# Weight folds moved into the first cross attention, the last down products over all PSUM banks, and Fourier blocks in another order

## The chip, the cores and the metric

One core of one Trainium2 chip runs the whole program in one launch. The metric is the device time of one execution in microseconds (us). The kernel before took 2213.67 us as the median of 3 runs (2210.46 to 2213.92). Engines are named as in the profile: PE is TensorE, DVE is VectorE, ACT is ScalarE, POOL is GpSimd, and SP (SyncE) issues every DMA of this kernel.

## The reference, cut to what matters

Two requests (512 and 256 tokens, width 1024) pass through two layers with the same weights. Each layer is a mixer, a cross attention over 256 memory tokens and a gated feed-forward part; layer 0's mixer is differential attention, layer 1's is a Fourier mixing.

```python
def fourier_mix(xn, w_in, w_out):
    u = (xn @ w_in).reshape(B, S, FNET_GROUPS, FNET_GROUP_DIM)
    f = jnp.fft.fft2(u, axes=(1, 3), norm="ortho").real
    return f.reshape(B, S, D_MODEL) @ w_out

def conv_glu(xn, w_up, conv_w, conv_b, w_down):
    gate, val = jnp.split(xn @ w_up, 2, axis=-1)
    gate = dwconv3(gate, conv_w, conv_b)          # 3 taps over time
    return (jax.nn.gelu(gate) * val) @ w_down

for i in range(2):
    x = x + mixer[i](rmsnorm(x, norm_mix_g[i]))
    x = x + cross_attention(rmsnorm(x, norm_xattn_g[i]), rmsnorm(mem, norm_mem_g[i]), ...)
    x = x + conv_glu(rmsnorm(x, norm_ffn_g[i]), ...)
return rmsnorm(x, final_norm_g)
```

## The kernel before, in words

Activations lie with channels on the partitions: 8 chunks of 128 channels by 768 tokens (both requests side by side, GROUPS = 512 and 256). Every float32 operand is split into a high and a low part, and a product is three matmuls (`mm3`, L150 to L155: high by high, low activation, low weight). A split is one ACT cast for the high part and one DVE subtraction for the low part (`load_w`, L147 and L148; `split`, L186 and L187).

The program is written in the order of the stages, and a scheduler then sets the order of the instructions on each engine from that order, from the buffers of each pool and from its own estimates. Each engine, and SP's DMA queue, works its list off in order: an instruction that waits holds all behind it.

The stages, in order: attention; cross attention 0 (`xq` queries, `xs` scores, `xt` transposes, `xav` values); its output product with the residual (`ob`, function `residual`); feed-forward 0 (`fp`, `fg`, `fv` up products, `fd` down products); the Fourier stage; cross attention 1; its output product; feed-forward 1, which ends in the final norm.

A feed-forward part takes its 22 hidden chunks in four blocks (6, 6, 6, 4). `prepare` loads the two up weights of a chunk and forms weight sums in tiles of tag `S` (two buffers, `s23` and `s14`) so that 7 quarter products do the work of 8. `first_half`, `rest` and `close` run these products and end in the hidden chunk (`hh`, `hl`). After a block come its down products, 8 output chunks `n` in each of the two token groups. In the first three blocks `fd` uses the two banks of tag `s`, and the result is scaled by DVE (`t`, L633) and added by POOL (`xs`, L634). In the last block (`last`), all eight weights are loaded ahead, the 512-token group is done for n = 0 to 7 and then the 256-token group; each result goes to `xr` (L629), and `each` squares it for the statistics of the next norm. For layer 0 `each` also starts to fold the activations for the Fourier stage (`into_mixer`, DVE ops `xm`, `eo`, `x3l`); for layer 1 it writes the output (`into_output`, L1270). The PSUM banks of this stage are b1, b2, b3 and s, two each; the statistics and their broadcast (`pt`, `pbmix`, `pbfin`) take banks of tag `s` too.

The weights of the Fourier stage are folded on the chip: sums and differences of left and right halves go to DRAM. `fold_weights` (L943 to L993) is a generator with 16 units: 8 of `in_fin` (names `fw..i`) and 8 of `in_fout` (`fw..o`). A unit loads two tiles of 256 KB, adds (L985) and subtracts (L986) on DVE and stores the results; for the five parts in `FIRST` it also splits them (L963, L964). It takes its tiles from tag `S` of feed-forward 0, and one step is taken before each `down` of the first three blocks (L656).

The Fourier stage opens with three products at once (`fu00`, `fu01`, `fu10`), then loads tables, then `fu11`, then the middle column `uny`, and later `fu20` and `fu21`. These products and `uny` share four PSUM banks (tag `g`).

Of the kernel before, what the change touches and what calls it, by code (L numbers as in the profile page):

```python
# [10 lines left out]
F32 = mybir.dt.float32  # L11
# [48 lines left out]
def trunk_kernel(ctx: ExitStack, tc: tile.TileContext, a: dict):  # L60
# [286 lines left out]
    def cross_attention(layer, acts, finish, pq, po):  # L347
        with tc.tile_pool(name=f"xa{layer}", bufs=1, reuse_waits="tile") as pool:
# [82 lines left out]
            for h, u in units + [(None, None)]:  # L431
                now = None
                if h is not None:
                    if h not in heads:
                        run(fill)
                        fill = chain(query(2 * h + 2), query(2 * h + 3)) if h < XA_HEADS - 1 else iter(())
                        heads[h] = load_head(h)
                    now = h, u, softmax(h, u, heads[h][0])
                run(fill, XSLICES[0])
                if prev is not None:  # L440
                    pt = transposed(*prev)
                run(fill, XSLICES[1])
                if prev is not None:
                    values(*prev[:2], pt, heads[prev[0]][1])
                run(fill, XSLICES[2])
                prev = now
            return o
# [12 lines left out]
    class Forms:  # L460
# [17 lines left out]
        def feed(self, pool, stats, gcol):  # L478
# [29 lines left out]
    def ffn(layer, pool, forms, extra, hidp, finish, x_src, x_keep, make_last, side):  # L508
# [115 lines left out]
        def down(n, w, j0, j1, x, off, ln, last, each):  # L624
            sl = slice(off, off + ln)
            ps = pss(f"fd{layer}_{j0}{n}_{off}")
            gemm(ps[:, :ln], w, [hid(j) for j in range(j0, j1)], sl)
# [13 lines left out]
        for b, (j0, j1) in enumerate(FF_BLOCKS):  # L641
# [8 lines left out]
            if not last:  # L650
                for n in range(KC):
                    w = load(n, j0, j1)
                    x = small_tile("xs", f"xs{b}{n}", T, 2)
                    nc.sync.dma_start(out=x, in_=(x_src if b == 0 else x_keep)[n])
# [266 lines left out]
    def attend_and_feed(layer, acts, finish, x_in, p_in, p_alt, make_last):  # L921


        with banks(f"xa{layer}", g=4, c=2, s=2):
            o = cross_attention(layer, acts, finish, p_alt, p_in)
            outer = ffn_pools[layer].enter_context(tc.tile_pool(name=f"ffo{layer}", bufs=1, reuse_waits="tile"))
            extra = lambda name, dtype=F32R: outer.tile([P, T], dtype, tag="xe", name=f"{name}{layer}", bufs=10)
            xe = [extra(f"xe{i}_") for i in range(10)]
            st = Stats(f"f{layer}")
            forms = Forms(layer, p_alt, p_in, xe)  # L930
            with tc.tile_pool(name=f"xo{layer}", bufs=1, reuse_waits="tile") as pool:
                residual(lambda name: pool.tile([P, T], F32, tag="xr", name=name, bufs=3), f"ob{layer}_",
                         lambda n: a["xo"][layer, n], o, lambda n: x_in[n], x2_scr[layer],
                         forms.feed(pool, st, V_FFN + 8 * layer))
        with ffn_pools[layer], banks(f"ffn{layer}", b1=2, b2=2, b3=2, s=2):
            pool = ffn_pools[layer].enter_context(tc.tile_pool(name=f"ffn{layer}", bufs=1, reuse_waits="tile"))
            hidp = [(page(p_in, f"hh{layer}_{i}"), page(p_in, f"hl{layer}_{i}")) for i in range(7)]
            return ffn(layer, pool, forms, extra, hidp, st.finish, x2_scr[layer], x2_scr[layer], make_last,
                       iter(()) if layer else fold_weights(pool))

    ffn_pools = [ExitStack(), ExitStack()]


    FIRST = ((0, 0), (0, 1), (1, 0), (1, 1), (2, 0))

    def fold_weights(pool):

        def pair(name, shape):
            t = pool.tile([P, KC, P], F32, tag="S", name=f"fw{name}", bufs=2)
            return t[:, :KC // 2], t[:, KC // 2:]  # L950

        def load(name, left, right):
            shape = list(left.shape)
            l, r = pair(f"lr{name}", shape)
            nc.sync.dma_start(out=l, in_=left)
            nc.sync.dma_start(out=r, in_=right)
            return l, r

        def keep(t, hi, dst, parts):
            if parts is None:  # L960
                return [(dst, t)]
            hi = hi.bitcast(F32R)
            nc.scalar.copy(out=hi, in_=t)  # L963
            nc.vector.tensor_tensor(out=t.bitcast(F32R), in0=t, in1=f32(hi), op=ALU.subtract)  # L964
            move(parts[0], hi)
            return [(parts[1], t)]
# [12 lines left out]
        yield  # L979
        now = load(units[0][0], *units[0][3])  # L980
        yield
        for k, (name, dst, parts, _) in enumerate(units):
            l, r = now
            e, hi = pair(f"e{name}", list(l.shape))
# [3 lines left out]
            stores = keep(e, hi, dst[0], parts[0]) + keep(l, r, dst[1], parts[1])  # L988
            yield
            for to, t in stores:  # L990
                move(to, t)
            if k + 1 < len(units):
                now = load(units[k + 1][0], *units[k + 1][3])  # L993
# [65 lines left out]
    with banks("fnet", g=4, s=4):  # L1059
        with tc.tile_pool(name="fnet", bufs=1, reuse_waits="tile") as pool:  # L1060
# [70 lines left out]
            mixed_in(1, 1)  # L1131
# [71 lines left out]
            mixed_in(2, 0)  # L1203
# [184 lines left out]
```

## Time and profile before

| | |
|---|---|
| median of 3 runs | 2213.67 us |
| profiled execution, its own time | 2211.7 us |
| its span | 2209.9 us |
| PE busy | 2077.9 us (94%) |
| DVE busy | 1372.8 us (62%) |
| ACT busy | 898.5 us (41%) |
| POOL busy | 576.1 us (26%) |
| granted TensorE clock, mean | 0.972 |

The busy time of an engine counts its instructions, not its issue of DMAs or its waits. The granted clock is 1 at TensorE's upper level (2.4 GHz) and 0.5 at the lower (1.2 GHz); a value between is a mean over a stretch. Times in rows are us from the start of the span.

### The profile page before, as it was taken

To read this page: it belongs to the slowest core of one execution; us is meant where nothing else is said; L and a number is where in the kernel's file an instruction comes from. 1 tells how busy PE (TensorE), PEld (TensorE's weight loads), DVE (VectorE), ACT (ScalarE), POOL (GpSimd) and SP (SyncE) were. 2 spreads that over 40 slices of the span, in tenths; PEclk is the share of its full clock that TensorE was granted. 3 is DMA by queue.
4 is the path that set the end of the run, shared out by engine and by line. 5 is a ranking of instruction groups with operands and counts; after the bars stand their busy time and mean duration, and the time that the engine had idled before them with its cause. 6 is when DMAs were issued, how large, how long until landed. Compare 5 with 4: busy or idle time off the path is not lost.

```text
span 2209.9 us, 32686 instructions
## 1 busy us (share of the span) xinstructions
PE 2077.9 (94%) x12455; PEld 1911.6 (87%) x12455; DVE 1372.8 (62%) x2226; ACT 898.5 (41%) x1550; POOL 576.1 (26%) x467
## 2 busy tenths in 40 slices
PE   7999999999999999928999987999999999999996
PEld 5898889799898899828999886889989989999895
DVE  6445777775435688537658466473567847748564
ACT  4324555554325455204325243353445524425232
POOL 5543222221200431202132324020033223142233
PEclk9999999999999999968999999999999999999997
DMA  5775686775532322752342454354242243241441
GB/s 185 211 228 166 209 261 210 246 243 202 191 104 93 118 91 73 262 209 86 129 158 72 134 168 142 127 185 149 77 146 82 72 141 110 79 169 67 133 154 62
DMA packets 151517, 328.35 MB, mean 149 GB/s; under 512 B 15680, under 2 KB 57792, under 8 KB 151360
## 3 DMA queue, kind: packets, MB, share of 16 engines
q1 hardware_dynamic: 151360, 326.26, 44.5%
q8 instruction: 98, 1.61, 0.3%
q14 instruction: 59, 0.48, 0.1%
HBM read 236.28 MB, written 89.92 MB: 148 GB/s over the span
## 4 chain that ended last, share of the span: by engine, by line
PE 47%; DVE 5%; DMA 3%; ACT 1%; issue 1%; POOL 1%; SPq 0%; DVEq 0%; POOLq 0%; ACTq 0%
PE fd L153 5%; PE fp L162 4%; PE fd L155 4%; PE fp L163 4%; PE fd L154 4%; PE fp L164 4%; PE fv L162 2%; PE fv L163 2%; PE fv L164 2%; PE fg L162 1%; PE fg L163 1%; PE fg L164 1%; PE xq L153 1%; PE xq L154 1%; PE xq L155 1%
## 5 line engine op out<-in xcount | busy, mean ns | idle before, releaser
L153 PE MATMUL fd<-hh,h_d 128*128 128x256 f32 (+1 forms) x640 | 221.4, 347 | 18.6 <-ACT hh L186 11.7
L154 PE MATMUL fd<-hl,h_d 128*128 128x256 f32 (+1 forms) x640 | 216.9, 341 | 0.0
L155 PE MATMUL fd<-hh,l_d 128*128 128x256 f32 (+1 forms) x640 | 214.0, 340 | 0.6 <-DVE l_d L148 0.5
L634 POOL TENSOR_TENSOR xs<-xs,t 128x512 f32<-128x512 f32 x96 | 119.5, 1245 | 274.9 <-DVE t L633 259.9
L153 PEld LDWEIGHTS fd<-hh,h_d 128*128 128x128 f32 x640 | 121.5, 190 | 43.2 <-ACT hh L186 12.5
L633 DVE TENSOR_TENSOR t<-fd,rbcf 128x512 f32<-128x512 f32 x96 | 53.3, 556 | 151.2 <-PE fd L155 95.4
L547 POOL TENSOR_TENSOR s<-r_v 128x512 f32<-128x512 f32 x44 | 57.9, 1316 | 316.1 <-DMA r_v<-in_up 250.3
L155 PEld LDWEIGHTS fd<-hh,l_d 128*128 128x128 f32 x640 | 121.7, 190 | 16.7 <-DVE l_d L148 2.7
L154 PEld LDWEIGHTS fd<-hl,h_d 128*128 128x128 f32 x640 | 121.9, 190 | 14.4 <-DVE hl L187 1.0
L147 ACT CAST h_d<-r_d 128x768 fp32r<-128x768 f32 (+1 forms) x56 | 44.5, 803 | 203.7 <-PE fd L154 180.3
L214 POOL TENSOR_TENSOR acc_x<-acc_x,sq_x 128x512 f32<-128x512 f32 (+2 forms) x49 | 66.9, 1371 | 186.4 <-ACT sq_x L213 186.4
L214 POOL TENSOR_TENSOR acc_f<-acc_f,sq_f 128x512 f32<-128x512 f32 (+1 forms) x28 | 35.1, 1259 | 291.6 <-issue 228.1
L826 POOL TENSOR_TENSOR p<-p 128x512 f32<-128x512 f32 (+1 forms) x48 | 58.2, 1213 | 176.9 <-DVE p L824 136.4
L548 POOL TENSOR_TENSOR s<-r_g,r_v 128x512 f32<-128x512 f32 x44 | 81.6, 1854 | 78.3 <-DVE l_C L187 78.3
L162 PE MATMUL fp<-bf,h_C 128*128 128x384 f32 x264 | 88.9, 337 | 0.4 <-ACT ux L589 0.4
L164 PE MATMUL fp<-bf,l_C 128*128 128x384 f32 x264 | 89.2, 338 | 0.0
L818 ACT ACTIVATE p<-sc,mx,rs 128x512 f32<-128x512 f32 (+1 forms) x96 | 67.1, 703 | 52.6 <-DVE mx L815 52.5
L163 PE MATMUL fp<-bf,h_C 128*128 128x384 f32 x264 | 88.5, 335 | 0.0
L601 DVE TENSOR_TENSOR hs<-fp,rbcf 128x128 f32<-128x128 f32 x88 | 27.4, 354 | 92.4 <-PE fp L164 92.4
L186 ACT CAST h_B<-s 128x1024 fp32r<-128x1024 f32 x44 | 46.1, 1048 | 83.3 <-DVE s L549 55.4
L186 ACT CAST h_A<-r_g 128x1024 fp32r<-128x1024 f32 x44 | 46.3, 1052 | 82.5 <-PE fg L163 48.6
L314 PE MATMUL xv<-h_xv,mnh 128*128 128x256 f32 x256 | 74.3, 290 | 0.0
(559 smaller groups left out, 7306.4 us busy)
## 6 DMA issues: line engine op xcount, KB each, us to landing
r_g<-in_up SPq DMA_DIRECT2D x44, 512.0 KB, 3.2
r_v<-in_up SPq DMA_DIRECT2D x44, 512.0 KB, 3.2
xs<-x_scr SPq DMA_DIRECT2D x48, 384.0 KB, 3.6
r_d<-in_down SPq DMA_DIRECT2D x48, 384.0 KB, 3.3
x_scr<-xs SPq DMA_DIRECT2D x48, 384.0 KB, 2.6
qst<-q_scr SPq DMA_DIRECT2D x64, 192.0 KB, 4.9
r_xk<-in_xk SPq DMA_DIRECT2D x16, 512.0 KB, 4.6
r_xv<-in_xv SPq DMA_DIRECT2D x16, 512.0 KB, 4.3
```

Source lines behind the costliest of these rows:

```text
L153: nc.tensor.matmul(out=ps, lhsT=wh, rhs=xh, start=first, stop=False)
L154: nc.tensor.matmul(out=ps, lhsT=wh, rhs=xl, start=False, stop=False)
L155: nc.tensor.matmul(out=ps, lhsT=wl, rhs=xh, start=False, stop=last)
L162: nc.tensor.matmul(out=ps, lhsT=wh, rhs=xh, start=first and p == 0, stop=False, skip_group_check=True)
L163: nc.tensor.matmul(out=ps, lhsT=wh, rhs=xl, start=False, stop=False, skip_group_check=True)
L164: nc.tensor.matmul(out=ps, lhsT=wl, rhs=xh, start=False, stop=p == 3, skip_group_check=True)
L186: nc.scalar.copy(out=hi, in_=src)
L214: nc.gpsimd.tensor_tensor(out=self.acc[:, sl], in0=self.acc[:, sl], in1=sq[:, :n], op=ALU.add)
L314: nc.tensor.matmul(out=ps, lhsT=xh[:, ts], rhs=wh[:, kc % 4, :], start=kc == 0, stop=False)
L548: nc.gpsimd.tensor_tensor(out=s23[:, h:], in0=a11, in1=a21, op=ALU.subtract)
L634: nc.gpsimd.tensor_tensor(out=x[:, sl], in0=x[:, sl], in1=t[:, :ln], op=ALU.add)
L818: nc.scalar.activation(p[:, c, :nk], scs[c][:, :nk], AF.Exp, bias=mx[:, c:c + 1], scale=rs8[:, tq:tq + 1], accum_out=sm[:, c, qc:qc + 1])
```

## The change

Three edits, and one clean-up without effect (`x_src` was the same tensor as `x_keep`).

First, `fold_weights` gets its list of units from outside, takes four tiles of its own (`fwl`, `fwr`, `fwe`, `fwh`, one buffer each) from whichever pool it is given, and is stepped twice in each turn of cross attention 0's loop (12 units) and once per result of the output product (4 units). Feed-forward 0 no longer steps it.

Second, the last block's down products of a token group hold eight banks at once (s, s, b1, b1, b2, b3, b2, b3). In the 512-token group the first six chunks do three of their four hidden chunks first, and the last hidden chunk afterwards.

Third, in the Fourier stage `mixed_in(1, 1)` and `mixed_in(2, 0)` are called before the tables are loaded.

```diff
-            units = [(h, u) for h in range(XA_HEADS) for u in range(3)]
+            steps = [(h, u) for h in range(XA_HEADS) for u in range(3)]
+            side = fold_weights(pool, units)
+            for h, u in steps + [(None, None)]:
+                next(side, None)
...
                 run(fill, XSLICES[1])
+                next(side, None)
...
             def each(n, xn, off, ln):
                 pair = n // 2
+                next(side, None)
                 stats.add(xn[:, off:off + ln], off, ln)
...
                     for off, ln in GROUPS:
-                        next(side, None)
                         down(n, w, j0, j1, x, off, ln, False, None)
...
+            order = ("s", "s", "b1", "b1", "b2", "b3", "b2", "b3")
+            hids = [hid(j) for j in range(j0, j1)]
             for off, ln in GROUPS:
-                for n in range(KC):
-                    down(n, ws[n], j0, j1, xr[n], off, ln, True, each)
+                ps = [None] * KC
+                early = 6 if off == 0 else 0
+                for part in (0, 1):
+                    for n in range(KC):
+                        k0, k1 = (0, j1 - j0 - 1) if part == 0 else (j1 - j0 - 1, j1 - j0)
+                        if n >= early:
+                            if part == 0:
+                                continue
+                            k0 = 0
...
+                        for k in range(k0, k1):
+                            mm3(ps[n][:, :ln], (ws[n][0][:, k, :], ws[n][1][:, k, :]),
+                                [t[:, sl] for t in hids[k]], k == 0, k == j1 - j0 - 1)
+                        if part:
+                            down(n, ws[n], j0, j1, xr[n], off, ln, True, each, ps[n])
...
+        def tile_(tag, name, dtype=F32):
+            return pool.tile([P, KC // 2, P], dtype, tag=tag, name=f"{tag}{name}", bufs=1)
...
+        for name, dst, parts, src in units:
+            flush()
+            l, r = tile_("fwl", name), tile_("fwr", name)
+            nc.sync.dma_start(out=l, in_=src[0])
+            nc.sync.dma_start(out=r, in_=src[1])
+            yield
+            e = tile_("fwe", name)
             nc.vector.tensor_tensor(out=e, in0=l, in1=r, op=ALU.add)
             nc.vector.tensor_tensor(out=l, in0=l, in1=r, op=ALU.subtract)
+            keep(e, f"{name}e", dst[0], parts[0])
+            keep(l, f"{name}o", dst[1], parts[1])
             yield
...
+            mixed_in(1, 1)
+            mixed_in(2, 0)
             hid_t = table("dft_h", [NHID])
...
-            mixed_in(1, 1)
...
             hidden(0)
-            mixed_in(2, 0)
             mixed_in(2, 1)
```

What this does to the order is shown at three places. The first is SP's queue in cross attention 0, in the changed kernel; the names with `fw` are tiles of the fold, `kt` and `vt` are keys and values of a head, `r_xq` a query weight.

```order
L986 DMA fwri00_7128<-in_fin 128x512
L68 DMA kt0_00_7131<-xk_scr0_86 128x2x512
L68 DMA vt0_00_7133<-xv_scr0_88 128x4x256
L68 DMA kt0_01_7135<-xk_scr0_86 128x2x512
L68 DMA vt0_01_7137<-xv_scr0_88 128x4x256
L68 DMA fin3_scr_90<-fwhi00e_7193 128x512
L68 DMA fin3_scr_90<-fwei00_7190 128x512
L986 DMA fwri04_7207<-in_fin 128x512
L68 DMA kt0_10_7431<-xk_scr0_86 128x2x512
L68 DMA fin3_scr_90<-fwhi00o_7197 128x512
L68 DMA fin3_scr_90<-fwli00_7127 128x512
L68 DMA vt0_10_7433<-xv_scr0_88 128x4x256
```

The loads of the heads, which stood one behind another, now have stores of the fold between them, each of which waits for its DVE or ACT result.

The second is PE at the last down products of feed-forward 0; `hh0_0` and `hl0_0` are the last hidden chunk, `hh0_4` to `hh0_6` the three before it, and `fd0_180_0` to `fd0_187_0` the eight output chunks. Before:

```order
L155 MATMUL fd0_181_0_13250<-hh0_6_8756,l_d0_181_13197 128x512
L153 MATMUL fd0_180_0_13235<-hh0_0_8744,h_d0_180_13189 128x512
L153 MATMUL fd0_181_0_13250<-hh0_0_8744,h_d0_181_13196 128x512
L154 MATMUL fd0_180_0_13235<-hl0_0_8745,h_d0_180_13189 128x512
L155 MATMUL fd0_180_0_13235<-hh0_0_8744,l_d0_180_13190 128x512
L154 MATMUL fd0_181_0_13250<-hl0_0_8745,h_d0_181_13196 128x512
```

After:

```order
L155 MATMUL fd0_181_0_13271<-hh0_6_8940,l_d0_181_13223 128x512
L153 MATMUL fd0_182_0_13281<-hh0_4_8936,h_d0_182_13229 128x512
L154 MATMUL fd0_182_0_13281<-hl0_4_8937,h_d0_182_13229 128x512
L155 MATMUL fd0_182_0_13281<-hh0_4_8936,l_d0_182_13230 128x512
L153 MATMUL fd0_182_0_13281<-hh0_5_8938,h_d0_182_13229 128x512
```

Before, two output chunks are brought up to the last hidden chunk and the third matmul row shown already needs it; now chunks 182 to 185, nine matmuls each, come first. Feed-forward 1 is moved in the same way.

The third is PE in the Fourier stage, at the end of `fu11`. Before:

```order
L155 MATMUL fu11_13890<-x3h7_13181,fi3wlo_13567 128x388
L153 MATMUL uny_13919<-x3h0_13167,nywh_13880 36x388
L154 MATMUL uny_13919<-x3l0_13168,nywh_13880 36x388
L155 MATMUL uny_13919<-x3h0_13167,nywl_13881 36x388
L153 MATMUL uny_13919<-x3h1_13169,nywh_13880 36x388
```

After:

```order
L155 MATMUL fu11_13900<-x3h7_13207,fi3wlo_13593 128x388
L153 MATMUL fu20_13927<-x3h0_13193,fi4whi_13746 128x388
L154 MATMUL fu20_13927<-x3l0_13194,fi4whi_13746 128x388
L155 MATMUL fu20_13927<-x3h0_13193,fi4wlo_13747 128x388
L153 MATMUL fu20_13927<-x3h1_13195,fi4whi_13746 128x388
```

`fu20`, 24 matmuls, stands where `uny` stood, and `uny` follows it; the order of ACT's casts and of SP's loads up to there is as before.

## Rows read from the trace of the kernel before

**Rows 1.** Waits of PE: engine, line, waited for: us in total, times, longest us.

```profile
PE fp L162 <- ACT h_B L186: 46.1, 1, 46.1
PE fd L153 <- ACT hh L186: 11.7, 2, 6.1
PE fd L153 <- DVE xr L629: 5.7, 5, 1.8
```

**Rows 2.** Timeline before 1004 us: start, us, instruction [idle before <-releaser].

```profile
990.78 0.69 DVE L985 TENSOR_TENSOR fweo<-fwlro 128x512 f32<-128x512 f32 x1 [4.68 <-DMA fwlro<-in_fout]
...
997.21 0.69 DVE L985 TENSOR_TENSOR fweo<-fwlro 128x512 f32<-128x512 f32 x1 [5.01 <-DMA fwlro<-in_fout]
...
1000.30 1.26 POOL L547 TENSOR_TENSOR s<-r_v 128x512 f32<-128x512 f32 x1 [50.13 <-DMA fout_scr<-fweo]
```

**Rows 3.** Stretches, both feed-forwards: width, busy by engine (instructions), PEclk, DMA share, GB/s.

```profile
774.61:1323.62 549.01, 489.39 (x2727) 461.75 (x2728) 360.07 (x478) 198.56 (x264) 137.84 (x101) 0.94 0.41 138
1668.47:2160.04 491.57, 484.92 (x2728) 459.16 (x2728) 331.35 (x436) 192.81 (x254) 138.07 (x101) 0.99 0.34 113
```

**Rows 4.** Stretches: down products of block 0, feed-forward 0 and 1.

```profile
885.05:948.66 63.61, 57.88 (x312) 49.34 (x313) 36.85 (x51) 14.81 (x21) 18.46 (x15) 0.97 0.78 269
1779.26:1835.10 55.84, 55.66 (x314) 48.13 (x313) 23.65 (x31) 8.90 (x11) 21.42 (x17) 1.00 0.49 168
```

**Rows 5.** Stretches of cross attention 0 and of its output product.

```profile
610.00:670.00 60.00, 60.00 (x380) 54.06 (x380) 23.61 (x48) 17.80 (x39) 0.00 (x0) 1.00 0.25 87
...
680.00:690.00 10.00, 10.00 (x84) 9.69 (x83) 7.93 (x24) 6.34 (x20) 0.00 (x0) 1.00 0.29 100
...
720.00:730.00 10.00, 10.00 (x57) 8.69 (x56) 8.75 (x11) 6.32 (x9) 5.07 (x4) 1.00 0.51 187
```

**Rows 6.** DMA issues of the fold: KB each, median us from issue to landing.

```profile
fwlri<-in_fin SPq DMA_DIRECT2D x16, 256.0 KB, 3.4
...
fout_scr<-fweo SPq DMA_DIRECT2D x8, 256.0 KB, 2.1
```

**Rows 7.** Timeline of POOL and DVE in the output product.

```profile
738.20 1.33 POOL L501 TENSOR_TENSOR F<-F 128x384 f32<-128x384 f32 x1
...
738.69 1.25 DVE L502 TENSOR_TENSOR F<-F 128x384 f32<-128x384 f32 x1
...
754.02 0.56 DVE L500 TENSOR_TENSOR F<-F 128x384 f32<-128x384 f32 x1 [1.37 <-ACT F L495]
```

**Rows 8.** Timeline of DVE and PE at the last down products, feed-forward 0.

```profile
1318.63 0.69 DVE L148 TENSOR_TENSOR hl<-r_d,hh 128x512 fp32r<-128x512 f32 x1 [0.25 <-ACT hh L147]
...
1323.62 1.22 PE L153 MATMUL fd<-hh,h_d 128*128 128x512 f32 x2 [6.10 <-ACT hh L186]
...
1328.30 0.40 PE L153 MATMUL fd<-hh,h_d 128*128 128x512 f32 x1
...
1342.89 0.39 PE L153 MATMUL fd<-hh,bf 128*128 128x512 f32 x1
```

**Rows 9.** Stretches after the wait for the last hidden chunk, and of the activations' fold.

```profile
1323.62:1343.78 20.16, 20.16 (x80) 15.69 (x81) 5.78 (x8) 4.42 (x7) 7.64 (x6) 0.91 0.13 38
...
1349.77:1368.84 19.07, 10.68 (x76) 9.45 (x74) 19.06 (x34) 8.21 (x20) 5.37 (x6) 0.98 0.88 302
...
2160.04:2180.11 20.07, 20.07 (x80) 15.61 (x81) 5.78 (x8) 4.42 (x7) 7.68 (x6) 0.92 0.00 1
```

**Rows 10.** Timeline of DVE near the end of the program.

```profile
2190.00 5.36 DVE L1270 SCALAR_TENSOR_TENSOR xr<-xr,vec,pbfin 128x512 f32<-128x512 f32 x8
...
2198.44 0.42 DVE L629 TENSOR_TENSOR xr<-fd,xr 128x256 f32<-128x256 f32 x1 [2.75 <-PE fd L155]
```

**Rows 11.** Timeline of SP and PE in the Fourier stage.

```profile
1395.43 0.38 SPq L68 DMA_DIRECT2D fi4wlo<-fin_scr  x1
...
1398.29 0.36 PE L153 MATMUL uny<-x3h,nywh 128*36 128x388 f32 x1 [4.58 <-DVE ul L187]
```

**Rows 12.** DMA issues: the weight of `fu20` (KB each, us to landing).

```profile
fi4wlo<-fin_scr SPq DMA_DIRECT2D x1, 512.0 KB, 4.9
```

More of the change, by code (lines that the diff above doesn't have):

```diff
@@ L344, in feed, with cross_attention @@
         return each
-    def cross_attention(layer, acts, finish, pq, po):
+    def cross_attention(layer, acts, finish, pq, po, units=()):
         with tc.tile_pool(name=f"xa{layer}", bufs=1, reuse_waits="tile") as pool:
@@ L446, in cross_attention @@
                 prev = now
+            run(1.0 for _ in side)
             return o
@@ L476, in form, with feed @@
             return out
-        def feed(self, pool, stats, gcol):
+        def feed(self, pool, stats, gcol, side):
             f, last = {}, {}
@@ L506, in feed, with ffn @@
             return each
-    def ffn(layer, pool, forms, extra, hidp, finish, x_src, x_keep, make_last, side):
+    def ffn(layer, pool, forms, extra, hidp, finish, x_keep, make_last):
         hs_buf = []
@@ L622, in hid, with down @@
             return hidp[j % 7]
-        def down(n, w, j0, j1, x, off, ln, last, each):
+        def down(n, w, j0, j1, x, off, ln, last, each, ps=None):
             sl = slice(off, off + ln)
-            ps = pss(f"fd{layer}_{j0}{n}_{off}")
-            gemm(ps[:, :ln], w, [hid(j) for j in range(j0, j1)], sl)
+            if ps is None:
+                ps = pss(f"fd{layer}_{j0}{n}_{off}")
+                gemm(ps[:, :ln], w, [hid(j) for j in range(j0, j1)], sl)
             if last:
@@ L653, in ffn @@
                     x = small_tile("xs", f"xs{b}{n}", T, 2)
-                    nc.sync.dma_start(out=x, in_=(x_src if b == 0 else x_keep)[n])
+                    nc.sync.dma_start(out=x, in_=x_keep[n])
                     for off, ln in GROUPS:
-                        next(side, None)
                         down(n, w, j0, j1, x, off, ln, False, None)
@@ L918, in trunk_kernel, with fold_units @@
     a_banks.close()
[L921 to L941, printed above, removed]
-    FIRST = ((0, 0), (0, 1), (1, 0), (1, 1), (2, 0))
[L946 to L966, printed above, removed]
+    FIRST = ((0, 0), (0, 1), (1, 0), (1, 1), (2, 0))
+    def fold_units():
         h = KC // 2
@@ L978, in fold_weights, with flush, keep @@
                           [a["fout"][n, :, i] for i in range(2)]))
[L979 to L984, printed above, removed]
+        return units
+    def fold_weights(pool, units):
+        stores = []
+        def flush():
+            for to, t in stores:
+                move(to, t)
+            stores.clear()
+        def tile_(tag, name, dtype=F32):
+            return pool.tile([P, KC // 2, P], dtype, tag=tag, name=f"{tag}{name}", bufs=1)
+        def keep(t, name, dst, parts):
+            if parts is None:
+                stores.append((dst, t))
+                return
+            hi = tile_("fwh", name, F32R)
+            nc.scalar.copy(out=hi, in_=t)
+            nc.vector.tensor_tensor(out=t.bitcast(F32R), in0=t, in1=f32(hi), op=ALU.subtract)
+            move(parts[0], hi)
+            stores.append((parts[1], t))
+        for name, dst, parts, src in units:
[5 more added lines that the diff above has]
+            e = tile_("fwe", name)
@@ L985, in fold_weights @@
             nc.vector.tensor_tensor(out=e, in0=l, in1=r, op=ALU.add)
             nc.vector.tensor_tensor(out=l, in0=l, in1=r, op=ALU.subtract)
-            stores = keep(e, hi, dst[0], parts[0]) + keep(l, r, dst[1], parts[1])
+            keep(e, f"{name}e", dst[0], parts[0])
+            keep(l, f"{name}o", dst[1], parts[1])
             yield
[L990 to L993, printed above, removed]
+        flush()
@@ new lines, in fold_weights, with attend_and_feed @@
+        yield
+    def attend_and_feed(layer, acts, finish, x_in, p_in, p_alt, make_last):
+        with banks(f"xa{layer}", g=4, c=2, s=2):
+            units = [] if layer else fold_units()
+            o = cross_attention(layer, acts, finish, p_alt, p_in, units[:12])
+            outer = ffn_pools[layer].enter_context(tc.tile_pool(name=f"ffo{layer}", bufs=1, reuse_waits="tile"))
+            extra = lambda name, dtype=F32R: outer.tile([P, T], dtype, tag="xe", name=f"{name}{layer}", bufs=10)
+            xe = [extra(f"xe{i}_") for i in range(10)]
+            st = Stats(f"f{layer}")
+            forms = Forms(layer, p_alt, p_in, xe)
+            with tc.tile_pool(name=f"xo{layer}", bufs=1, reuse_waits="tile") as pool:
+                side = fold_weights(pool, units[12:])
+                residual(lambda name: pool.tile([P, T], F32, tag="xr", name=name, bufs=3), f"ob{layer}_",
+                         lambda n: a["xo"][layer, n], o, lambda n: x_in[n], x2_scr[layer],
+                         forms.feed(pool, st, V_FFN + 8 * layer, side))
+                run(1.0 for _ in side)
+        with ffn_pools[layer], banks(f"ffn{layer}", b1=2, b2=2, b3=2, s=2):
+            pool = ffn_pools[layer].enter_context(tc.tile_pool(name=f"ffn{layer}", bufs=1, reuse_waits="tile"))
+            hidp = [(page(p_in, f"hh{layer}_{i}"), page(p_in, f"hl{layer}_{i}")) for i in range(7)]
+            return ffn(layer, pool, forms, extra, hidp, st.finish, x2_scr[layer], make_last)
@@ L995, in load_first @@
+    ffn_pools = [ExitStack(), ExitStack()]
     def load_first(b):
```

4 lines of the change are left out of this document (3 added, 1 removed).

## The prediction

> **What bounds the kernel now.** I read the engines' shares and the slices of the span first, then the waits of PE, then stretches of the span, then the timeline around each long wait. PE is busy 94% of the span, and nearly everything outside a few places is PE-bound, so the time moves with PE's waits and with the matmuls run at the lower clock. The list of waits [rows 1] has one entry that dwarfs the rest: 46.1 us in a single wait of `fp` for the weight sum `h_B`. The timeline before it [rows 2] shows why. POOL's `s`, which `h_B` is made from, had been idle 50.13 us until a store of the fold (`fout_scr<-fweo`) had landed: the fold and `prepare` share the two buffers of tag `S`. Meanwhile the fold went one unit every 6.43 us (990.78 to 997.21), DVE waiting some 5 us of each for its load. Next come the two waits for the last hidden chunk (11.7 us, one of 6.1) and the five waits for `xr` [rows 1].
>
> **The fold out of feed-forward 0.** Feed-forward 1 runs the same products without a fold, so it prices the removal without adding waits one by one. From the first waiting `fp` matmul to the wait for the last hidden chunk feed-forward 0 takes 549.01 us and feed-forward 1 491.57, with 2727 and 2728 matmuls [rows 3]: 57.44 longer. That holds the 46.1 us, the matmuls after it at the lower clock (granted mean 0.94 against 0.99), and the disturbed down products of block 0 (63.61 against 55.84, 7.77 longer [rows 4]). 6.10 of it against some 5.6 in feed-forward 1 is the wait for the last chunk [rows 1, 8], which belongs to the second edit; so 56.9 us go.
>
> **The fold into cross attention 0.** It brings 32 additions and subtractions and 10 splits: 42 DVE instructions of 0.69 us [rows 2], 29 us, with 10 ACT casts, and 32 loads and 42 stores in SP's queue. 34 of the DVE instructions fall into the attention, 8 into the output product. What covers them: from 610 to 670 us DVE is busy 23.61 of 60 us and PE never idle [rows 5], with query products between the scores, so there I count nothing. From 680 to 690 DVE is busy 7.93 of 10 [rows 5]; the order puts about two units, four instructions, into the 20 us of that dense part: 2.8 us of work against some 4 us of idle time, which do not fall together, so I count 1 us. A unit cannot go faster than load, two DVE instructions and store (3.4 + 1.4 + 2.1 = 6.9 us [rows 2, 6]), because its one buffer must be stored before the next load; where the order puts two units closer than that, DVE holds the softmax behind a load for 1 to 2 us. I take 3 us in all. The lower bound is 0. The upper bound is the nearest place where a fold ran beside products, block 0's down products: 7.77 us for about 6.5 units [rows 4], 1.2 a unit, 19 us for 16. I stay near the low end because the down products had two PSUM banks and the queries have four, and because PE there had no idle slice at all.
>
> One rule speaks against it. In the output product a DVE instruction on two SBUF tensors took 1.25 us just after POOL's `F` began, and 0.56 us with POOL free [rows 7]. The Trainium skill, "GPSIMD Engine Reference", section "1. Specifications", says that GpSimd shares its SBUF interfaces with VectorE and contends with instructions of two SBUF inputs; the trace agrees. By it the 8 fold instructions in the output product could take 0.69 us more each, 5.5 us of DVE time in a stretch where DVE is busy 8.75 of 10 at its worst [rows 5], and the 34 in the attention nothing, as POOL does nothing there (0.00). With four banks between PE and DVE I leave it inside the bounds above.
>
> **Last down products, feed-forward 0.** Four more output chunks, 36 matmuls, now stand before the first need of the last hidden chunk. A 512-column matmul takes (1342.89 - 1328.30) / 63 = 0.232 us [rows 8], so they cover 8.3 us of a wait of 6.10. The weight of the sixth chunk was split by 1318.63 + 0.69 [rows 8], before PE reaches it (1323.62 - 6.10 + 27 x 0.232 = 1323.8). The wait goes, and with it the lower clock behind it: 0.91 over 20.16 us [rows 9] is 1.8 us. In all 7.9 us earlier. What is late next: the fold of the activations, where DVE is busy 19.06 of 19.07 us while PE waits five times for `xr` [rows 1, 9]. The free banks let PE run ahead there, but DVE's work stays, so those 5.7 us become one longer wait. In the new order the last `xr` stands behind three DVE instructions more and the statistic `ms` behind three more; that returns about 1 us. Net 7; bounds 0 (DVE's chain given back whole) and 9.
>
> **Fourier blocks.** By its look `fu20` fills the 4.58 us that `uny` waits [rows 11]. But `uny` waits for a bank: the four banks hold `fu00` to `fu11`, and the first comes free when DVE has split `fu00`, behind the casts of the tables on ACT, whose order is unchanged. `fu20` is now the fifth user and waits for the same split, and also for its weight, which lands at 1395.43 + 4.9 = 1400.3 [rows 11, 12], 2.0 us after `uny` started. I take 1.5 of these 2.0 us lost, as the first matmuls need only the other half of the weight, which was issued just before; bounds 2 lost and 6 gained (the wait and the slow matmuls behind it gone).
>
> **Last down products, feed-forward 1.** The wait of 11.7 - 6.1 = 5.6 us [rows 1] goes, with 0.08 of 20.07 us at the lower clock [rows 9], 1.6. At the end the last chunk's result waited 2.75 us for PE [rows 10], because the bank it needed was held by the broadcast that the eight `L1270` instructions (5.36 us [rows 10]) read; chunks 6 and 7 now have banks of their own and are done by then. Together 10; bounds 6 and 12.
>
> **The sum**, against the profiled execution's own 2211.7 us: -56.9 + 3 - 7 + 1.5 - 10 = -69.4, so 2142.3. The median of the runs is 2.0 above that execution; I put the forecast between, at 2143.
>
> **Rivals.**
> A, the fold keeps its price: it delays the attention as it delayed block 0, 19 us instead of 3, 2159. For it: DVE and SP work in order, and a load held by a store holds everything behind. Against: the idle DVE of [rows 5].
> B, the bank edit is given back: DVE's chain sets both ends, so 7 are lost in feed-forward 0 and 7 of 10 in feed-forward 1 (only the 2.75 stay): 2157. For it: DVE at 19.06 of 19.07 [rows 9]. Against: that chain starts when the first group's statistics are done, and these come earlier.
> C, the Fourier edit does what it seems to: the wait of 4.6 and the slow matmuls behind it go, 7.5 better than forecast, 2135. Against: the shared banks.
> D, slower than before: every unit is exposed. SP holds the loads of the next head and of the output product behind fold stores, as the loads and POOL were held before 1004 us; each unit then costs its 6.43 us [rows 2], 16 units 103 us, and 2143 - 3 + 103 = 2243. It decides from (56.9 + 7 - 1.5 + 10) / 16 = 4.5 us a unit. Against: in that stretch PE had nothing else to run, here it has queries. The Trainium skill, "DMA: Bandwidth & Descriptors", section "Anatomy of one DMA", says that a semaphore wait of a DMA is made on the issuing sequencer before dispatch, so a store that waits does hold all later loads; no row here shows how long.
>
> **How the numbers follow.** Forecast 0.66, A 0.18, B 0.10, C 0.03, D 0.03. The forecast's own range, with the fold at 0 to 8 and the bounds near their middle, is 2136 to 2150. The range for 8 times in 10 reaches to A and B and leaves out D and the far side of C: 2133 to 2161. A measurement of this kernel tells about 0.2% (4.4 us) from no change: faster by more than that 0.96, within it 0.01, slower 0.03.
>
> **What would show it.** The wait of `fp` for `h_B` and POOL's 50 us before `s` gone, and feed-forward 0's stretch of [rows 3] near 492 us less its last wait: right. PE waits of `xs`, `xt` or `xav` for DVE summing over 8 us between 600 and 770 us: A. The two waits for `hh` gone; a wait of about 10 us for the second group's statistic before `fu00`, and `fu00` about 7 us nearer to `fd`'s start: right; `fu00` no nearer: B. A wait of `fu20` for `ul` or its load in place of `uny`'s: right; no wait there: C. The end, from the moment the last hidden chunk is there, about 4 us shorter than the 49.9 before (2209.9 - 2160.04 [rows 9]). The forecast is wrong if the fold makes waits that the attention cannot hide.

## The result and the profile after

The changed kernel took 2141.4 us (median of 4, 2140.87 to 2142.89), the kernel before beside it 2212.1: a ratio of 0.968 (0.9666 to 0.970). The forecast was 2143. The profiled execution has a span of 2139.9 us against 2209.9.

The waits of PE in the changed kernel (us in total, times, longest), against [rows 1]:

```profile
PE pt_x L227 <- POOL acc_x L214: 11.1, 1, 11.1
PE pt_fin L227 <- POOL acc_fin L214: 5.2, 1, 5.2
...
PE fu L153 <- DVE ul L187: 3.3, 1, 3.3
...
PE fu L155 <- DMA fi4wlo<-fin_scr: 1.3, 1, 1.3
...
PE xav L153 <- DVE xo0l L187: 1.2, 1, 1.2
...
PE xav L153 <- DVE pl L187: 1.0, 1, 1.0
PE ob L154 <- DVE xo0l L187: 0.8, 1, 0.8
```

The three waits of [rows 1] are gone: 46.1 us for `h_B`, 11.7 for `hh`, 5.7 for `xr`. New are the two waits for a statistic, 11.1 and 5.2.

Where the time went is read from five stretches, cut at the same instructions in both kernels: first `xq` to first `fp` (cross attention 0 and output product), to the last `fd` group (feed-forward 0), to the first `fu` (last down products), to the `xq` of layer 1 (Fourier stage), and from the last `fd` group of feed-forward 1 to the end. Columns as in [rows 3]. Before:

```profile
592.24:768.78 176.54, 176.02 (x1119) 157.70 (x1117) 89.09 (x168) 72.06 (x150) 24.16 (x20) 1.00 0.35 123
768.78:1313.89 545.11, 489.19 (x2737) 462.29 (x2736) 356.55 (x471) 197.23 (x262) 140.11 (x109) 0.95 0.40 135
1313.89:1370.70 56.81, 39.43 (x208) 32.36 (x208) 35.73 (x60) 19.94 (x40) 19.55 (x18) 0.92 0.56 188
1370.70:1484.08 113.38, 103.47 (x691) 100.07 (x690) 71.74 (x135) 52.90 (x98) 17.74 (x18) 0.97 0.41 142
...
2150.85:2209.90 59.05, 39.79 (x208) 33.12 (x207) 25.93 (x45) 12.54 (x23) 18.27 (x18) 0.81 0.22 78
```

After:

```profile
594.65:774.79 180.14, 176.66 (x1118) 157.75 (x1117) 113.95 (x210) 77.61 (x160) 22.12 (x20) 1.00 0.67 228
774.79:1261.13 486.34, 482.78 (x2737) 458.34 (x2736) 327.68 (x429) 191.62 (x253) 140.93 (x109) 1.00 0.33 112
1261.13:1310.54 49.41, 36.18 (x208) 31.43 (x208) 35.48 (x61) 19.74 (x40) 19.59 (x18) 0.90 0.64 216
1310.54:1423.95 113.41, 103.50 (x691) 100.59 (x690) 70.99 (x134) 52.44 (x97) 17.43 (x18) 0.97 0.41 141
...
2090.79:2139.90 49.11, 36.00 (x208) 31.29 (x207) 26.36 (x45) 13.46 (x24) 18.30 (x18) 0.90 0.27 95
```

| stretch | predicted | measured |
|---|---|---|
| cross attention 0, with the fold | +3 | +3.6 |
| feed-forward 0, without it | -56.9 | -58.8 |
| last down products, layer 0 | -7 | -7.4 |
| Fourier stage | +1.5 | 0.0 |
| last down products, layer 1 | -10 | -9.9 |
| the rest (not changed) | 0 | +2.5 |
| sum | -69.4 | -70.0 |

Of the last 2.5, 2.4 lie before the first `xq` and belong to the execution: `xq` begins between 589.99 (the run without the Fourier edit) and 595.21 (the changed kernel once more). So a term read from one profile is known to a microsecond or two, and that the sums agree to 0.6 us is partly luck: the five changed stretches alone give -72.5.

### The profile page after: what moved, and what is told of

Read it like the earlier page. It is cut to its first block, busy times and chain, and to the rows that moved or that the text cites. A ratio compares the mean times of both kernels' runs of the same rounds, so it can differ in the third digit from the quotient of the medians.

```text
span 2139.9 us, 32662 instructions
## 1 busy us (share of the span) xinstructions
PE 2067.6 (97%) x12455; PEld 1908.0 (89%) x12455; DVE 1367.6 (64%) x2226; ACT 898.0 (42%) x1550; POOL 575.3 (27%) x467
## 4 chain that ended last, share of the span: by engine, by line
PE 83%; DVE 7%; DMA 3%; ACT 2%; issue 2%; POOL 2%; SPq 0%; POOLq 0%; DVEq 0%; ACTq 0%
PE fd L153 5%; PE fp L163 5%; PE fp L162 5%; PE fp L164 5%; PE fd L155 5%; PE fd L154 5%; PE fv L162 3%; PE fv L163 3%; PE fv L164 3%; PE ob L154 2%; PE ob L153 2%; PE ob L155 2%; PE xq L153 2%; PE xq L154 2%; PE xq L155 2%
## 5 line engine op out<-in xcount | busy, mean ns | idle before, releaser
L186 ACT CAST h_C<-s 128x1024 fp32r<-128x1024 f32 x44 | 46.2, 1051 | 63.4 <-PE fp L163 61.5
```

The source lines that it names most:

```text
L186: nc.scalar.copy(out=hi, in_=src)
```

## The experiments

The first two do one edit alone. **The fold alone** (the kernel before with `fold_weights` moved):

```diff
+            side = fold_weights(pool, units)
+            for h, u in steps + [(None, None)]:
+                next(side, None)
...
-                        next(side, None)
...
+                side = fold_weights(pool, units[12:])
```

> The kernel before with the first edit alone: the fold in cross attention 0 and its output product, the last down products and the Fourier blocks as before. By the prediction's terms it is -56.9 + 3, so about 54 us faster than the kernel before (2158), the wait of fp for h_B gone and feed-forward 0 as long as feed-forward 1. If the fold kept the price of block 0's down products, 38 us faster (2174). If the second edit had a part in the 46 us wait, less than 50 us faster with a wait of fp left.

Measured: 2160.4 us, ratio 0.976 (0.9745 to 0.9778). The stretches of the attention and of feed-forward 0 are 181.02 and 486.99 us, so +4.5 and -58.1: the second edit had no part in the 46 us. Rival A's 2174 is out. The profiled execution was the slowest of the four (2165.1 us). What it has above the expected 2158 lies mostly in the two last down products, where this kernel is as before the change:

```profile
1262.19:1322.36 60.17, 41.79 (x209) 34.47 (x208) 35.72 (x60) 19.24 (x40) 19.55 (x18) 0.86 0.51 177
...
2102.33:2163.20 60.87, 40.27 (x208) 33.35 (x207) 26.43 (x45) 13.69 (x24) 18.24 (x18) 0.83 0.22 77
```

60.17 and 60.87 against 56.81 and 59.05; the two waits for `hh` were 14.0 us, not 11.7. Whether the other three executions had this too is not recorded. In layer 1 a weight load landed some 1.2 us later than before and held the ACT instruction of the hidden chunk behind its cast. So the exposed wait was longer in this execution; in the changed order there is no such wait.

**The banks alone** (the kernel before with the second edit, as in the diff of the change).

> The kernel before with the second edit alone. By the prediction's terms -7 in feed-forward 0 and -10 in feed-forward 1, so 17 us faster (2195), both waits of fd for hh gone. If DVE's chain sets both ends and gives the gain back, only the 2.75 us at the end stay (2209).

Measured: 2192.5 us, ratio 0.991 (0.9897 to 0.9926), with the wait for `h_B` still 46.2. The two stretches:

```profile
1313.83:1363.27 49.44, 36.18 (x209) 31.43 (x208) 35.51 (x61) 19.60 (x40) 19.62 (x18) 0.89 0.62 216
...
2142.49:2191.60 49.11, 36.01 (x208) 31.28 (x207) 26.38 (x45) 13.63 (x24) 18.30 (x18) 0.90 0.27 96
```

That is -7.4 and -9.9, as in the changed kernel. Rival B is out: DVE's chain did not give the gain back. The two edits add up (-52.2 and -20.1 by medians, -71 together).

**The order without the hand-written part.**

```diff
-                early = 6 if off == 0 else 0
+                early = 0
```

> The changed kernel with eight banks in the last down products but without the order written out for the first six chunks. In its order four chunks are brought up to the last hidden chunk, not two as before the change and not six. Two more chunks, 18 matmuls of 0.232 us, cover 4.2 of the 6.1 us. If the order is what removes the waits, 1.9 and 1.4 us of them stay, and the lower clock behind them costs up to 1.7 us in each layer: 4 to 7 us slower than the changed kernel (2145 to 2148). If the banks alone do it, the same time within 2 us.

Measured: 2145.8 us (2145.6 to 2148.5), 4.4 us slower than the changed kernel. Its waits and stretches:

```profile
PE fd L153 <- ACT hh L186: 4.5, 2, 2.4
```

```profile
1259.15:1311.03 51.88, 36.50 (x209) 31.24 (x208) 34.98 (x61) 19.07 (x39) 19.61 (x18) 0.89 0.60 206
2092.35:2144.30 51.95, 36.37 (x208) 31.12 (x207) 26.09 (x45) 13.64 (x24) 18.30 (x18) 0.88 0.26 90
```

2.5 and 2.8 us longer than with the order. So of the edit's 17.3 us the banks, which let the scheduler bring up four chunks, bring 12, and the written order 5.3.

**The Fourier edit undone.**

```diff
-            mixed_in(1, 1)
-            mixed_in(2, 0)
             hid_t = table("dft_h", [NHID])
...
+            mixed_in(1, 1)
...
             hidden(0)
+            mixed_in(2, 0)
```

> The changed kernel with the third edit undone, fu20 back behind uny. By the prediction's term 1.5 us faster (2140), the wait before uny 4.6 us as in the kernel before; that is below what a measurement tells, so the trace decides. If the third edit had filled the wait, 7.5 us slower (2149). If it does nothing, since the wait for the bank only changes its name, the same time within 1 us.

Measured: 2139.4 us (2136.9 to 2142.9), which a measurement cannot tell from 2141.4. The trace:

```profile
PE uny L153 <- DVE ul L187: 3.0, 1, 3.0
```

```profile
1306.45:1419.66 113.21, 104.85 (x692) 100.91 (x690) 70.99 (x134) 52.44 (x97) 17.43 (x18) 0.94 0.41 142
```

Without the edit PE waits 3.0 us for the bank; with it 3.3 for the same split and 1.3 for the weight, so the 1.5 us predicted are there as a wait in this pair. But PE's busy time is 104.85 us here and 103.50 with the edit, at a granted clock of 0.94 and 0.97, and the stretch is only 0.2 us shorter. Neither number can be put down to the edit: over all profiles of this record the stretch takes 111.1 to 115.4 us at a granted clock of 0.93 to 0.98 in nine profiles with the edit, and 112.6 to 113.5 at 0.94 to 0.97 in four with the old order (the candidate below left out). So the sign of the term stays open. Rival C, 7.5 us, is out.

**The fold twice**: the 12 units of cross attention 0 done twice.

```diff
-            o = cross_attention(layer, acts, finish, p_alt, p_in, units[:12])
+            again = [(f"x{u[0]}",) + u[1:] for u in units]
+            o = cross_attention(layer, acts, finish, p_alt, p_in, units[:12] + again[:12])
```

> The changed kernel with every unit of the fold done twice, the same values stored twice: 24 units in cross attention 0, 8 in the output product, so the extra 16 units have a price of their own in the same place. By the prediction another 3 us, up to 8 since the output product now takes two instead of one unit in each 10 us (2144 to 2149). If a unit kept the price of block 0's down products, 1.2 us each, 19 us more (2160). If each unit were exposed as before 1004 us, 6.43 us each, 103 us more (2244).

Measured: 2238.0 us (2237.0 to 2241.1), slower than the kernel before. The edit repeats only the 12 units of the attention; the output product still has 4, not the 8 that the expectation counts. My theory failed here: the 12 extra units cost 97 us, 8.1 each, more than the 6.43 at which rival D prices an exposed unit. One wait holds nearly all of it:

```profile
PE ob L153 <- DVE ob_x L332: 95.1, 1, 95.1
```

and SP's and DVE's timelines show what released it:

```profile
813.00 0.33 SPq L68 DMA_DIRECT2D fout_scr<-fwlxo  x1
813.38 0.44 SPq L327 DMA_DIRECT2D ob_x<-x_scr  x1
```

```profile
811.55 0.69 DVE L989 TENSOR_TENSOR fwexo<-fwlxo,fwrxo 128x512 f32<-128x512 f32 x1 [5.57 <-DMA fwlxo<-in_fout]
...
816.79 1.02 DVE L332 TENSOR_TENSOR ob_x<-ob,ob_x 128x512 f32<-128x512 f32 x2 [3.82 <-DMA ob_x<-x_scr]
```

The first 12 units ran from 600 to 715 us, as in the changed kernel (604 to 717): they fill the attention. The other 12 followed at 7.9 us each (95.1 / 12), with DVE idle between them, while the first load of `ob_x` stood in SP's queue behind the last store and its addition in DVE's list behind the last unit. In the changed kernel the first unit's addition begins at 604.18 and the twelfth's at 716.53, 10.2 us a unit, and the first use of `ob_x` follows with no wait of PE:

```profile
604.18 0.69 DVE L989 TENSOR_TENSOR fwei<-fwli,fwri 128x512 f32<-128x512 f32 x1 [2.50 <-DMA fwri<-in_fin]
...
716.53 0.69 DVE L989 TENSOR_TENSOR fweo<-fwlo,fwro 128x512 f32<-128x512 f32 x1 [0.37 <-issue]
...
722.36 1.02 DVE L332 TENSOR_TENSOR ob_x<-ob,ob_x 128x512 f32<-128x512 f32 x2 [0.15 <-DMA ob_x<-x_scr]
```

So the theory became: the fold is nearly free as long as its chain ends before the first `ob_x` is needed, and 12 units just fit. Four runs test that. One rival must be kept in mind: the loop of the attention steps the fold 26 times, two steps a unit, so from the fourteenth unit on the program writes the units behind the loop, and the order of writing alone might keep them out.

**All 16 units in the attention**, none in the output product; no work is added.

```diff
-            o = cross_attention(layer, acts, finish, p_alt, p_in, units[:12])
+            o = cross_attention(layer, acts, finish, p_alt, p_in, units)
-                side = fold_weights(pool, units[12:])
+                side = fold_weights(pool, ())
```

> The changed kernel with all 16 units of the fold in cross attention 0 and none in the output product: the same work, 4 units moved. With 12 units in the attention the last one ended at 718 us, where the output product needs its first ob_x, and PE did not wait for it. In the order of DVE and of SP the first ob_x stands behind all units. If the attention has no room left, the four units run after it one by one, 6.8 us each as between 690 and 717 us, less some 4 us that the four banks allow: PE waits about 23 us for ob_x (2161 to 2166). If there is still room, the time stays (2141), or falls by 1 to 2 us since the output product is then free of the fold.

Measured: 2169.5 us (2167.8 to 2172.7), 28.8 more than the changed kernel beside it (2140.7). The wait and DVE's last units:

```profile
PE ob L153 <- DVE ob_x L332: 26.2, 1, 26.2
```

```profile
719.15 0.69 DVE L989 TENSOR_TENSOR fweo<-fwlo,fwro 128x512 f32<-128x512 f32 x1 [1.07 <-DMA fwlo<-in_fout]
727.02 0.69 DVE L989 TENSOR_TENSOR fweo<-fwlo,fwro 128x512 f32<-128x512 f32 x1 [4.27 <-DMA fwlo<-in_fout]
733.77 0.69 DVE L989 TENSOR_TENSOR fweo<-fwlo,fwro 128x512 f32<-128x512 f32 x1 [5.34 <-DMA fwlo<-in_fout]
740.84 0.69 DVE L989 TENSOR_TENSOR fweo<-fwlo,fwro 128x512 f32<-128x512 f32 x1 [5.64 <-DMA fwlo<-in_fout]
746.02 1.02 DVE L332 TENSOR_TENSOR ob_x<-ob,ob_x 128x512 f32<-128x512 f32 x2 [3.77 <-DMA ob_x<-x_scr]
```

The four units cost 7.2 us each by the medians. PE ran out of other work at 720.53 us (the wait ends at 746.77), as the thirteenth unit's two DVE instructions ended (the second at 720.56); DVE was idle for a load 4 to 5.6 us of each of the last three. So the attention has no room for four more. Thirteen alone were not run; by this trace the thirteenth should cost less than those after it.

**Two buffers for the doubled fold**, and **two buffers for the changed kernel's fold** (the same edit; in the attention only):

```diff
-            side = fold_weights(pool, units)
+            side = fold_weights(pool, units, 2)
...
-            return pool.tile([P, KC // 2, P], dtype, tag=tag, name=f"{tag}{name}", bufs=1)
+            return pool.tile([P, KC // 2, P], dtype, tag=tag, name=f"{tag}{name}", bufs=bufs)
```

> The kernel with every unit folded twice, but with two buffers for each of the fold's four tiles in cross attention 0 (one in the output product, as before). There PE waited 95.1 us for the first ob_x, since 12 units filled the attention and the load of ob_x stood in SP's queue behind the stores of 12 more, which went on alone at 7.9 us each. Theory 1: the pace of a unit is the chain through its one buffer (load, two DVE instructions, store), so with two buffers about 24 units fit into the 120 us and the wait falls below 20 us (2145 to 2165). Theory 2: the pace is set by SP's queue, where a store that waits for DVE holds the next load whatever the buffers; then the wait stays above 60 us (over 2200). In between, the wait falls as the pace does.

Measured: 2173.2 us, 65 less than with one buffer; the wait for `ob_x` is 21.0 us:

```profile
PE ob L153 <- DVE ob_x L332: 21.0, 1, 21.0
```

The first and the twentieth unit on DVE:

```profile
598.56 0.69 DVE L989 TENSOR_TENSOR fwei<-fwli,fwri 128x512 f32<-128x512 f32 x1 [1.31 <-DMA fwri<-in_fin]
...
721.74 0.69 DVE L989 TENSOR_TENSOR fwexi<-fwlxi,fwrxi 128x512 f32<-128x512 f32 x1
```

With two buffers the units come 6.5 us apart ((721.74 - 598.56) / 19) and twenty fit where twelve did, though the last seven of them are written behind the loop. So the one buffer set the pace and kept the later units out, not SP's order as such and not the order of writing. Theory 2 is out; theory 1 holds in kind and misses its bounds, by a microsecond for the wait and by 8 for the time.

> The changed kernel with two buffers for each of the fold's tiles in cross attention 0. The fold costs about 3.6 us there (the stretch from xq to the first fp matmul is 180.1 us against 176.5 without a fold). If what it costs is DVE held behind a load that its one buffer delayed, the stretch falls to 177 to 178 us and the kernel by 2 to 3 us (2139). If it is DVE's added work, the stretch stays at 180 (2141).

Measured: 2144.0 us (2141.2 to 2144.9), and the attention's stretch 183.92 us, not 177 to 178. Neither expectation came: the stretch became longer. Where all units fit, the second buffer gains nothing; a wait of `xs` for `xq0l` of 5.3 us came instead. On PE the 3.6 us of the changed kernel are 3.0 of waiting (for `xo0l` and `pl`, in the list of waits above) and 0.6 of busy time; why DVE was late there was not found.

**The fold's DMAs on POOL's queue**, with the doubled fold:

```diff
-                move(to, t)
+                nc.gpsimd.dma_start(out=to, in_=t)
...
-            nc.sync.dma_start(out=l, in_=src[0])
+            nc.gpsimd.dma_start(out=l, in_=src[0])
...
```

> The kernel with every unit folded twice (one buffer), the loads and stores of the fold issued by POOL instead of SP; the order of all other instructions is unchanged. PE waited 95.1 us there for ob_x. If it was SP's queue that held the load of ob_x behind fold stores, that load now goes early and the wait falls below 30 us (under 2175). If it is DVE's list, where ob_x stands behind the additions of all extra units, the wait stays near 95 (2230 to 2245), although the load of ob_x is there long before.

Measured: 2292.7 us (2288.2 to 2294.1), outside both ranges. The load of `ob_x` now goes early, and PE waits all the same:

```profile
761.91 1.33 SPq L327 DMA_DIRECT2D ob_x<-x_scr  x3
```

```profile
859.89 0.69 DVE L989 TENSOR_TENSOR fwexo<-fwlxo,fwrxo 128x512 f32<-128x512 f32 x1 [6.59 <-DMA fwlxo<-in_fout]
861.23 1.02 DVE L332 TENSOR_TENSOR ob_x<-ob,ob_x 128x512 f32<-128x512 f32 x2
```

```profile
PE ob L153 <- DVE ob_x L332: 108.2, 2, 102.8
```

So SP's hold, which rival D named, is not needed for it: DVE's list alone suffices, where the first `ob_x` stands directly behind the last unit. That the kernel got 55 us slower still, with new waits of `xt` and `xav` inside the attention, I did not follow further.

**A candidate**: the Fourier edit undone, and the statistics of the 256-token group ahead of other DVE work, in both layers.

```diff
-                if 2 <= n:
-                    for c in ((0,), (1, 2), (3,), (4, 5), (6,), (7,))[n - 2]:
-                        fold(0, c)
+                if n in (4, 6):
+                    fold(0, n // 2 - 2)
...
-            if off and n == 5:
-                write(*GROUPS[0])
+            if off and n == 6:
+                write(*GROUPS[0], range(2))
             if off and n == KC - 1:
+                write(*GROUPS[0], range(2, KC))
                 st.finish(GROUPS[1:])
```

> A candidate: the changed kernel with the third edit undone, and with the statistics of the 256-token group ahead of other DVE work in both layers. In feed-forward 0 the activations' fold of chunks 3 to 7 comes after the last xr instead of between them; in feed-forward 1 two of the eight output instructions of the 512-token group stay ahead of the xr of chunk 6 and six go behind that of chunk 7. Where pt_x waits 11.1 us and pt_fin 5.2 us now, DVE stood before the statistic. If that is so, about 2 us at the end and 2 to 3 us before fu00, with nothing from the Fourier order: 4 to 5 us faster than the changed kernel (2137). If DVE's whole chain sets both places whatever its order, the same time as the changed kernel.

Measured: 2140.6 us (2138.6 to 2143.0), no difference. The end became 3.1 us shorter, but the other half gave that back in an unexpected way. The wait for `pt_x` fell to 1.9 us and `fu` began 14.7 us after `pt_x` instead of 24.8. Yet `uny` came 57.5 us after `pt_x`, against 51.1 in the kernel with the Fourier edit undone, whose order of products is the same. The stretch from the first `fu` to `uny`, in two pieces, in the candidate:

```profile
1297.54:1321.00 23.46, 18.68 (x84) 16.20 (x83) 21.61 (x47) 10.09 (x29) 6.21 (x12) 0.65 0.30 121
1321.00:1340.29 19.29, 19.29 (x88) 19.23 (x88) 5.89 (x10) 6.15 (x11) 0.00 (x0) 0.56 0.56 190
```

and in the kernel with the Fourier edit undone:

```profile
1306.45:1319.00 12.55, 12.55 (x90) 12.55 (x88) 11.37 (x27) 6.25 (x19) 6.04 (x12) 0.81 0.01 3
1319.00:1332.79 13.79, 10.78 (x83) 10.45 (x81) 2.86 (x6) 4.02 (x8) 0.00 (x0) 0.96 0.55 172
```

In the candidate PE started earlier, waited in short pieces for DVE and ACT (18.68 of 23.46 us busy), and ran at a granted clock of 0.65 and then 0.56; after one long wait it ran at 0.81 and 0.96. The same products and their wait took 42.75 us instead of 26.34. Only a part of that is waiting. In both kernels the last matmuls of the three first products are 72 narrow ones (130 columns), with PE busy throughout. Two microseconds of them in the candidate and in the other kernel:

```profile
1325.00:1327.00 2.00, 2.00 (x12) 2.00 (x11) 0.70 (x1) 0.54 (x1) 0.00 (x0) 0.50 0.39 129
```

```profile
1319.00:1321.00 2.00, 2.00 (x21) 2.00 (x19) 0.31 (x1) 0.00 (x0) 0.00 (x0) 1.00 0.74 248
```

In the candidate they came at a granted clock of 0.50, to which it had fallen after waits of 1.63 and 0.86 us near 1311, and took 15.3 us (1318.99 to 1334.25); in the other kernel they came at 1.00 and took 8.0 (1317.34 to 1325.33). The candidate's clock rose again only in the products behind them. That is one execution of each.

**The end alone**: the changed kernel with the candidate's second half.

> The changed kernel with the edit of the candidate that helped, alone: at the end of feed-forward 1 two of the eight output instructions of the 512-token group stay ahead of the xr of chunk 6, and six go behind that of chunk 7. In the candidate the stretch from the last down products to the end took 46.0 us instead of 49.1, while its other edit gave 3.6 us back before the cross attention. So 3 us faster than the changed kernel run beside it (about 2138), the wait of pt_fin 2.1 instead of 5.2 us. If the end is set by DVE's whole work, no difference.

> The changed kernel once more, unaltered, beside the kernel with the edit at the end alone: 2141 within 2 us, and the same waits of PE as in its first profile.

Measured on the same chip: 2136.4 us (2135.1 to 2138.3) against 2140.7 (2138.3 to 2143.2) for the changed kernel; ratios to the kernel before 0.966 (0.9646 to 0.9677) and 0.968 (0.9664 to 0.9697). The last stretch:

```profile
2087.03:2133.30 46.27, 36.00 (x208) 31.28 (x207) 25.93 (x45) 12.75 (x23) 18.36 (x18) 0.89 0.28 100
```

46.27 us against 49.11: 2.8 of the 4.3 us by medians, the rest is within what runs differ. The wait of `pt_fin` is 2.1 us, as expected. In the changed kernel eight `L1297` instructions, 5.35 us, stood on DVE before the last two `xr`:

```profile
2122.37 5.35 DVE L1297 SCALAR_TENSOR_TENSOR xr<-xr,vec,pbfin 128x512 f32<-128x512 f32 x8
2127.64 0.74 DVE L635 TENSOR_TENSOR xr<-fd,xr 128x256 f32<-128x256 f32 x2
```

This kernel has the lowest median of all that ran. The intervals of the two ratios overlap, so it is the stretch that shows the gain. The unaltered kernel's second profile has the long waits of the first; its attention takes 182.34 us instead of 180.14, and its wait of `fu` for `ul` is 1.7 us instead of 3.3.

## Why the prediction was right

**Fold out of feed-forward 0.** Feed-forward 1 was the right price: cut in the same way it takes 488.43 us in the changed kernel, where feed-forward 0 takes 486.34. The term came out as -58.8, and -58.1 alone, against -56.9.

```profile
1602.36:2090.79 488.43, 484.60 (x2737) 459.46 (x2736) 328.15 (x429) 191.79 (x253) 141.04 (x109) 0.99 0.34 111
```

**Fold into cross attention 0.** The size held: seven runs with this placing have 179.4 to 182.3 us in that stretch and the two without a fold 176.5, so 2.9 to 5.8 against the 3 predicted. (The upper bound was priced a little low: the stretch of block 0 holds the additions of 6 units, not 6.5, so 1.3 us a unit and 21 us for rival A.) The reason given held only in part. DVE rose from 89.09 to 113.95 us of busy time in the stretch and PE waited 3.0 us for it, so idle DVE time did cover the work. But idle time is not the condition: in the runs with one buffer DVE stood idle for some 5 us of each exposed unit, and the extra units cost 7.2 and 8.1 us each. The condition is that the chain of units, 10.2 us apart inside the attention, ends before the output product's first `ob_x`. The prediction did not set the units against the length of the attention. Its own 6.9 us a unit would have misled it: some 17 units would have seemed to fit the 120 us from the first unit to `ob_x`, and 16 did not. That the placing put 12 there and not 16 was luck, as far as the prediction goes. Rival D, given 0.03, is a real mechanism that this placing escapes by fewer than four units. The rule of the Trainium skill cited for it ("DMA: Bandwidth & Descriptors", "Anatomy of one DMA") agrees with SP's rows of the doubled fold, where the load of `ob_x` goes 0.38 us after the last store; the run with POOL's queue shows that it is not the whole of the hold.

On the rule of the Trainium skill ("GPSIMD Engine Reference", "1. Specifications") the trace agrees in the one place of eight where it could: beside POOL's `F` an addition took 1.34 us.

```profile
743.62 1.02 POOL L506 TENSOR_TENSOR F<-F 128x384 f32<-128x384 f32 x1
743.85 1.34 DVE L989 TENSOR_TENSOR fweo<-fwlo,fwro 128x512 f32<-128x512 f32 x1 [1.96 <-DMA fwlo<-in_fout]
```

The other seven took 0.68 or 0.69, and in the timeline POOL ran nothing beside them. So by the rule the fold cost 0.65 us here, not 5.5.

**Last down products.** Both terms held, in the changed kernel and alone, and so did the next thing late: one wait of 11.1 us for the second group's statistic, with `fu` 7.4 us nearer to `fd`. One sign was mis-stated: from the last hidden chunk to the end I expected about 4 us less than 49.9. In the changed kernel its cast ends at 2100.80, so it is 39.1. The work that fills the wait is missing behind it, so nearly all of the gain appears there.

**Fourier blocks.** The wait moved from `uny` to `fu20` and to its load, as predicted. The size was below what can be read: in the one pair of profiles 1.6 us of wait came and 1.35 us of PE's busy time went, the medians are 2.0 us apart in the predicted direction, and both lie within what executions differ. So the mechanism is shown and the sign of the term is not.

## What to carry to other kernels

Side work in a list that engines take in order is nearly free only if its chain ends before the first instruction that stands behind it is needed: divide the length of the covering stage by the time of one unit as measured inside that stage (here 10.2 us, not the 6.9 of the bare chain), count the units, and don't go by idle time. A second buffer shortens the unit. Where PE waits for the last operand, put other work ahead of it in banks of its own, and then look at which statistic waits next and what stands before it on DVE. Twice the same product in the program, once with the disturbance and once without, prices a removal better than adding up waits.

## What the hardware showed

In one pair of executions one long wait cost less than many short ones. In the candidate PE was busy for all of 19.29 us at a granted clock of 0.56, after a stretch of short waits, while the same products ran at 0.81 and 0.96 behind one wait of 11.1 us. The 72 narrow matmuls kept, busy all the time, the level at which they came: 0.21 us each at 0.50, 0.11 at 1.00. Work pulled forward into a stretch where it can only trickle can so come out later than if PE had waited; that the short waits alone did it is not shown by a run of its own. As an issuer of transfers POOL was slower than SP, 0.55 us of its time for each where SP took 0.33 to 0.44 in the rows above (timeline of POOL with the fold on its queue):

```profile
740.40 0.55 POOL L966 DMA_DIRECT2D fout_scr<-fwlo  x1 [0.37 <-DVE xo0l L187]
```
